# Order of the first expert-weight transfers, and place of one modulation block, in a three-stage block of attention and experts

## The chip, the cores and the metric

One core of a Trainium2 chip runs the whole program. The metric is the device time of one execution in microseconds (us); less is better.

## The reference

For 256 tokens of width 1024 the program computes two layers of a first kind and one of a second kind. Each layer is a mixer (several kinds of attention) followed by a mixture of 16 experts:

```
for l in range(2):
    h = layer_norm(ALPHA * h + mixer(h))
    h = layer_norm(ALPHA * h + grouped_moe(h))
mod = silu(c) @ w_ada + b_ada            # 6 rows of 1024: shifts, scales, gates
x = h + g1 * mixer2(rms(h) * (1 + sc1) + sh1)
x = x + g2 * hier_moe(rms(x) * (1 + sc2) + sh2)
```

An expert layer gives each token two of the 16 experts, and for each expert computes

```
y = y + gate[:, e] * ((silu(h @ w_gate[e]) * (h @ w_up[e])) @ w_down[e])
```

with three 1024x512 float32 weights per expert (2 MiB each, 96 MiB a layer). `w_ada` is 1024x6144 (24 MiB); its product does not depend on `x`, so its 12 column blocks of 512 can be computed anywhere ahead of the third layer.

## The kernel before

**Stages.** The program is one long straight line of instructions per engine, in the order in which the Python code calls them: mixer 1, experts 1, mixer 2, experts 2, mixer 3, experts 3. Below, *expert stage 1, 2, 3* means these three `moe` calls.

**An expert stage** (`moe`, L955) works on eight pairs of experts. The router (`router1`, L856, for stages 1 and 2; `router2` for stage 3) ends in a mask on DVE. TensorE then counts positions (`ppos`, `pcnt`), and `gather(0)` (L979) picks the tokens of the first two pairs into `xT`. At L1127 every engine reads an overflow flag and branches over a rare path (`overflow`, L1124). Then, for each pair, `expand(pr, 0)` multiplies by the gate weights, `expand(pr, 1)` by the up weights (both L1026: 32 matmuls each, written as 64 PE records for a pair), `shrink` by the down weights of the pair before (L1073), and `scatter` adds the result to `yacc`. Inside an `expand` the two experts alternate and `k` runs from 0 to 7; the first half of the weights of an expert holds k = 0 to 3, the second half k = 4 to 7.

**The weight transfers.** `moe_loads` (L916) lists 96 jobs of 1 MiB: for pair 0 gate (jobs 0 to 3), pair 0 up (4 to 7), pair 1 gate (8 to 11), pair 1 up (12 to 15), pair 0 down (16 to 19), pair 2 gate (20 to 23) and so on; in each four the order is first halves of both experts, then second halves. All are issued by the SP queue in list order. `MOE_SEQ` (L39) names for each job the pool its tile comes from, `w` (13 buffers), `b`, `r` or smaller ones; `q`, which only job 3 has, means four pieces of 256 KiB in the small pool `m2` (5 buffers). A transfer whose buffer is still in use waits on the SP queue, and all later transfers wait behind it.

`LATE` (L35) takes a job out of the list and puts it in at another position: job 3 (second half of the second expert's gate in pair 0) stands behind job 21 in stages 1 and 2, and behind job 20 in stage 3. `load(n)` issues the list up to position n: `load(5)` in the mixer (letter `5` of `FILL`), `load(8)` in the third mixer, and `load(22)` or `load(21)` (`MOE_FIRST`, L38) in `moe` ahead of the branch. After the branch the rest follows pair by pair (L1119).

**The buffers of jobs 16 to 19** in stages 1 and 2 come free with the last modulation blocks, because those blocks' weight tiles (`wa`, two of 1 MiB for a block) lie in the same pool `w`.

**The modulation blocks.** `ada` (L1234) is a generator; each step computes one 512-column block: 16 PE matmuls (`pada`, L1244), one ACT copy of the result into the second `wa` tile (L1264), and a small transfer from that tile to DRAM on the POOL queue (L1254). So a block's first `wa` tile is free when the matmuls have read it, the second one when the small transfer has landed. `ada_step` (L1285), at the start of each block, issues a queued follow-up: a small POOL transfer (`adac`, L1272) or two short DVE sums (`total`, L1275).

**The mixer's heads.** `pipe` (L468) goes through 20 attention heads of mixers 1 and 2 and takes filler steps between them (1.1 a head, 22 in all, the rest afterwards). `FILL` (L30) is the order of the fillers of the two mixers: projections (`q k v c f g h`), loads (`5 x a`), one output-projection step for the first 128 tokens (`o`, four matmuls L541), one modulation block (`A`), one output-projection step for the other tokens (`p`). Mixer 1 has four blocks and three `A`, mixer 2 has five blocks and four `A`. The one block that is left is computed after the router by `next(fill, None)` in `run`, followed by `warm(4)` (L117: bf16 matmuls on constants that keep TensorE at work) while the router's chain runs on DVE:

```
            mask, gates = self.router1(pr)
            self.to_tok(h1T, yacc[:, 1, :], 1, ALPHA, "a", "s")
            next(fill, None)
            self.warm(4)
```

Of the kernel before, what the change touches and what calls it, by code (L numbers as in the profile page):

```python
# [26 lines left out]
TABLES = "natural_log_exp_and_others"  # L27
WPOOL = 3
OUT = ("bbbr", (), (0, 1, 2, 3)), ("wwbr", (0, 1), (2, 3))
FILL = ("qkvcfgh5xaoAoAoAopppp", "qkvcfgh5xaoAoAoAoApppp")  # L30
PT1 = "to"
AHEAD = 6
KMC, FLG = (1, 3), 3
EXT, EXT2 = 0, 0
LATE = (3, 21), (3, 20)  # L35
PARTS = {"r": "rr", "x": "r4", "y": "44", "z": "422", "q": "2222"}
GATHER = (1, 3, 5)
MOE_FIRST = 22, 21  # L38
# [9 lines left out]
class Net:  # L48
# [523 lines left out]
    def mixer(self, l, hT, parts, W, ada, mid, tr, load):  # L572
# [64 lines left out]
        def tok(n, dst):  # L637
            pv = self.ps("ptok", "a")
            yield from self.tok3(n, parts, [(pv[:, i * S:(i + 1) * S], i, i == 0) for i in range(2)])
            self.evac(dst.rearrange("p i f -> p (i f)"), pv)  # L640
            yield
# [17 lines left out]
        def fox_qk(n, t, sc):  # L659
            pd = self.ps("pfq", "a")  # L660
            yield from self.proj3(n, parts, [(pd[:, j * S:(j + 1) * S], j * P, P, j == 0) for j in range(2)])
            for j in range(4):
                h = slice(j % 2 * 64, j % 2 * 64 + 64)
                self.evac(fox["QKf"][0:64, t, j, :], pd[h, j // 2 * S:j // 2 * S + S], sc)
            yield
# [5 lines left out]
        def filler():  # L671
# [4 lines left out]
                     "g": lambda: fox_qk("fk", 1, None), "h": lambda: tok("fv", fv)}  # L676
            for step in FILL[l]:
                if step in steps:
# [1160 lines left out]
    def run(self):  # L1839
        A, nc = self.A, self.nc  # L1840
        self.loads()
        c = self.c
        W = self.mixer_loads(0)
        nc.scalar.preload_act_table_set("silu_and_others")
        hT, hp = self.ln_in()
        for l in range(2):
            nc.gpsimd.tensor_scalar(c["qg", l], c["qg", l], 96 ** -0.5, None, op0=ALU.mult)
        self.wstream([(n, W[n]) for n in WSTREAM])
        self.wahead(2)
        tr = iter(())  # L1850
        for l in range(2):
            fill = self.ada(ADA_MX[l], W["ada"])
            h1 = []
            g, b = c["ln1_g", l], c["ln1_b", l]
            pr, parts = [], []

            def mid(xn):

                h1.append(self.big([P, 8, S], "h1T"))
                self.to_T(xn[:, 0], h1[0], g, b, 0)  # L1860
                self.warm(2)
                parts.append(self.parts())
                self.split_hi(xn, parts[0], 0)
                pr.append(self.ps("prt", "o"))
                self.router_mm(h1[0], c["rw"], 16, pr[0], 0)
                self.warm(3)

            We = lambda e: (A["exp_w_gate"][l, e], A["exp_w_up"][l, e], A["exp_w_down"][l, e])
            loads = self.moe_loads(We, MOE_SEQ[0], LATE[0])
            xn = self.mixer(l, hT, hp, W, fill, mid, tr, loads[0])  # L1870
            h1T, pr, parts = h1[0], pr[0], parts[0]
            self.split_lo(xn, parts, 0)
            self.split_hi(xn, parts, 1)
            self.to_T(xn[:, 1], h1T, g, b, 1)
            yacc = self.big([P, 2, D], "yacc")
            self.to_tok(h1T, yacc[:, 0, :], 0, ALPHA, "a", "s")
            self.warm(2)
            self.router_mm(h1T, c["rw"], 16, pr, 1)
            self.split_lo(xn, parts, 1)
            self.dbg(f"h1T{l}", h1T)  # L1880
            mask, gates = self.router1(pr)

            self.to_tok(h1T, yacc[:, 1, :], 1, ALPHA, "a", "s")
            next(fill, None)
            self.warm(4)
            xn2, sts = [], []

            def last(i, n):
                if i == 0 and n == 0:
                    xn2.append(self.big([P, 2, 8, P], "xn2"))  # L1890
                if n == 0:
                    sts.append(self.stats())
                nc.vector.bn_stats(sts[i][:, n, :], yacc[:, i, n * 512:(n + 1) * 512])
                if n == 1:
                    self.ln_rest(yacc, i, self.ln_scale(sts[i], LNE), xn2[0], "aa" if i == 0 else "av")

            self.moe(0, loads, parts, g, b, mask, gates, We, yacc, None, last, fill)
            Wa = self.ada_loads(ADA_TR[l:l + 1])
            W = self.mixer_loads(1) if l == 0 else self.mixer2_loads()
            fill = self.ada(ADA_TR[l:l + 1], Wa, "s", l == 0)  # L1900
            hT = self.big([P, 8, S], "h2T")
            next(fill)
            if l == 0:
                hp = self.hparts()
                self.wstream([(n, W[n]) for n in WSTREAM])
                for i in range(2):
                    self.to_T(xn2[0][:, i], hT, c["ln2_g", l], c["ln2_b", l], i, "ta"[i])
                next(fill)
                for i in range(2):
                    self.hl_tile(hT, hp, i)  # L1910
                tr = fill
                self.wahead(2)
            else:
                sq = self.big([P, 8, S], "sq2")
                self.wstream([(n, W[n]) for n, _ in WIN2_TILES])
                for i in range(2):
                    self.to_T(xn2[0][:, i], hT, c["ln2_g", l], c["ln2_b", l], i, "ta"[i])
                    self.square2(hT, sq, i)
                hp = self.hparts()
                self.wahead(2)  # L1920
                self.rms2(hT, sq, hp, fill)
        We = lambda e: (A["w1_2"][0, e], A["w3_2"][0, e], A["w2_2"][0, e])
        loads = self.moe_loads(We, MOE_SEQ[1], LATE[1])
        xt, parts, h3T, pr, g2b = self.mixer2(hT, hp, W, loads[0])
        self.dbg("x1", xt)
        self.dbg("h3T", h3T)
        mask, gates = self.router2(pr)

        def last(i, n):
            s = slice(n * 512, (n + 1) * 512)  # L1930
            nc.sync.dma_start(self.out[0, i * P:(i + 1) * P, s], xt[:, i, s])

        self.moe(1, loads, parts, self.mcol[:, 4, :], self.mcol[:, 3, :], mask, gates, We, xt, g2b, last)
# [150 lines left out]
```

## Time and profile before

| | |
|---|---|
| median of 3 runs | 1238.4 us (1237.06 to 1243.48) |
| the profiled execution's own time | 1240.28 us |
| its span, first to last instruction | 1238.6 us |
| mean granted TensorE clock | 0.976 |
| TensorE matmul records | 1161.9 us busy, 94% of the span |
| VectorE, ScalarE, GpSimd | 42%, 31%, 20% of the span |
| bytes moved by DMA | 395.46 MB, mean 319 GB/s |
| expert stages, first `expand` to last `shrink` | 191.6 to 401.2, 578.8 to 787.3, 1023.9 to 1230.2 us |

PE is the matmul row of TensorE, PEld its weight loads, DVE, ACT and POOL are the vector, scalar and GpSimd engines, SP the engine that only issues transfers (SPq its queue). A name like `pz<-we,xT` says that the instruction writes tile `pz` and reads `we` and `xT`. In square brackets stands the idle time of the engine before an instruction, and what ended it. PE busy time is modelled (matmuls overlap), so what PE loses is read from its idle times and from how long a known group of matmuls took.

### The profile page before, as it was taken

Reading aid. Unit: us, or ns where it says so; the run is one execution under the profiler, and the core shown is the slowest. Engines: PE = TensorE matmul, PEld = TensorE weight load, DVE = VectorE, ACT = ScalarE, POOL = GpSimd, SP = SyncE. Lnnn points to the kernel's source line nnn. Section 1 sums busy time; section 2 is a strip of 40 time slices with the busy share of each in tenths; the row PEclk is TensorE's granted clock in tenths of the full one; section 3 lists DMA queues with packets and bytes.
Section 4 is the critical chain, followed back from the end, with each engine's and each line's share of the span. In section 5 each row is a group of like instructions: output and inputs, shape, how many; then the busy total and the mean of one; then the engine's idle time right before and its main releaser. Section 6 shows DMA issues by size and latency. Waiting matters only on the chain. (4 is left out here: it accounts for less than half of the span.)

```text
span 1238.6 us, 16671 instructions
## 1 busy us (share of the span) xinstructions
PE 1161.9 (94%) x6366; PEld 673.6 (54%) x6366; DVE 517.1 (42%) x1135; ACT 381.4 (31%) x799; POOL 245.6 (20%) x356
## 2 busy tenths in 40 slices
PE   5999897999999799997999999899899989999997
PEld 4887453434344688645344343489898453434432
DVE  6565351212232756535023221565985360223323
ACT  5545341111111655424011011465464340101100
POOL 4655200000000356320000000132473200000000
PEclk9999898999999999999999999889899998999999
DMA  9814958999999964677999999984354267999995
GB/s 383 338 65 186 399 185 327 408 404 413 414 416 414 419 256 138 248 263 295 378 405 415 413 415 414 418 321 154 114 194 172 102 263 312 415 414 416 415 417 232
DMA packets 77947, 395.46 MB, mean 319 GB/s; under 512 B 7936, under 2 KB 9592, under 8 KB 49440
## 3 DMA queue, kind: packets, MB, share of 16 engines
q1 hardware_dynamic: 73488, 384.66, 78.2%
q0 software_dynamic: 2608, 7.73, 1.6%
q10 hardware_dynamic: 1760, 1.89, 0.5%
q8 instruction: 53, 0.87, 0.3%
q14 instruction: 38, 0.31, 0.1%
HBM read 389.41 MB, written 6.51 MB: 320 GB/s over the span
## 5 line engine op out<-in xcount | busy, mean ns | idle before, releaser
L1026 PE MATMUL pz<-we,xT 128*64 128x512 f32 x1536 | 343.9, 604 | 19.8 <-DMA we<-in_exp_w_gate 12.3
L1026 PEld LDWEIGHTS pz<-we,xT 128*64 128x64 f32 x1536 | 110.8, 139 | 239.6 <-issue 217.8
L1073 PE MATMUL py<-wd,aT 128*64 128x512 f32 x768 | 171.1, 593 | 0.9 <-DMA wd<-in_w 0.9
L1035 DVE TENSOR_TENSOR act<-sil,pz 128x512 f32<-128x512 f32 x24 | 16.5, 688 | 327.8 <-PE pz L1026 302.8
L1050 POOL TENSOR_SCALAR m_ge<-m_s 64x1 f32<-64x1 f32 x48 | 11.9, 247 | 586.5 <-DVE m_s L1045 339.9
L1073 PEld LDWEIGHTS py<-wd,aT 128*64 128x64 f32 x768 | 56.6, 137 | 110.2 <-issue 105.6
L1030 ACT ACTIVATE sil<-pz 128x512 f32<-128x512 f32 x24 | 14.3, 597 | 217.8 <-PE pz L1026 217.8
L1079 ACT ACTIVATE yh<-py,m_ge 128x512 fp32r<-128x512 f32 x32 | 22.0, 688 | 187.6 <-PE py L1073 187.6
L1080 DVE SCALAR_TENSOR_TENSOR yl<-py,m_ge,yh 128x512 fp32r<-128x512 f32 x32 | 24.0, 751 | 96.3 <-ACT yh L1079 96.3
L541 PE MATMUL pout<-w_o,oT 128*128 128x512 f32 x128 | 58.2, 602 | 0.0
L986 PE MATMUL pg<-G,xhi 128*128 128x256 f32 x192 | 47.8, 290 | 2.0 <-DVE G L975 2.0
L448 POOL TENSOR_SCALAR E<-E,r 128x128 f32<-128x128 f32 x40 | 31.6, 791 | 77.4 <-DVE r L444 77.2
L986 PE MATMUL pg<-G,xlo 128*128 128x256 f32 x192 | 46.7, 283 | 0.0
L1085 ACT ACTIVATE yh<-yf 128x512 fp32r<-128x512 f32 x16 | 10.1, 631 | 104.0 <-DVE yf L1084 104.0
L1099 PE MATMUL psc<-yh,GT 128*128 128x512 f32 x96 | 39.3, 410 | 1.1 <-ACT yh L1085 0.8
L1101 DVE TENSOR_TENSOR yacc<-yacc,psc 128x512 f32<-128x512 f32 x64 | 40.1, 680 | 0.0
L1099 PE MATMUL psc<-yl,GT 128*128 128x512 f32 x96 | 38.5, 401 | 1.3 <-DVE yl L1080 0.6
L541 PEld LDWEIGHTS pout<-w_o,oT 128*128 128x128 f32 x128 | 23.8, 194 | 26.0 <-issue 25.6
L986 PEld LDWEIGHTS pg<-G,xhi 128*128 128x128 f32 x192 | 36.7, 191 | 2.4 <-issue 1.6
L986 PEld LDWEIGHTS pg<-G,xlo 128*128 128x128 f32 x192 | 36.8, 191 | 0.0
L442 ACT ACTIVATE E<-s,nm 128x128 f32<-128x128 f32 (+1 forms) x48 | 20.2, 421 | 47.9 <-DVE nm L441 45.6
L1244 PE MATMUL pada<-wa,cz 128*32 128x512 f32 x192 | 24.2, 618 | 8.4 <-DVE yacc L1101 4.5
(512 smaller groups left out, 2122.4 us busy)
## 6 DMA issues: line engine op xcount, KB each, us to landing
wd<-in_exp_w_down SPq DMA_DIRECT2D x58, 1024.0 KB, 16.3
we<-in_exp_w_up SPq DMA_DIRECT2D x54, 1024.0 KB, 13.1
we<-in_w SPq DMA_DIRECT2D x52, 1024.0 KB, 15.0
we<-in_exp_w_gate SPq DMA_DIRECT2D x48, 1024.0 KB, 11.7
wd<-in_w SPq DMA_DIRECT2D x29, 1024.0 KB, 15.3
wa<-in_p_ada SPq DMA_DIRECT2D x24, 1024.0 KB, 15.2
we<-in_exp_w_gate SPq DMA_DIRECT2D x28, 512.0 KB, 13.7
we<-in_w SPq DMA_DIRECT2D x22, 512.0 KB, 14.8
```

The lines of the kernel that those rows point to most:

```text
L442: nc.scalar.activation(E[:, s], sc[:, s], AF.Exp, bias=nm[:, i:i + 1], accum_out=sm[:, i:i + 1])
L448: self.nc.gpsimd.tensor_scalar(E[:, 0:P], E[:, 0:P], r[:, 0:1], None, op0=ALU.mult)
L541: self.nc.tensor.matmul(acc, oT[:, cc, i * P:(i + 1) * P], w[cc][:, n * 512:(n + 1) * 512], start=(cc == 0), stop=(cc == 7), skip_group_ch ...
L986: nc.tensor.matmul(pg[:, :256], part[:, i, k, :], Gq[q][:, i].rearrange("p e s -> p (e s)"), start=(n == 0), stop=(n == 3))
L1026: nc.tensor.matmul(pz[64 * e:64 * e + 64, :], x[:, k, o + 64 * e:o + 64 * e + 64], w[e][k], start=(k == 0), stop=(k == 7), skip_group_chec ...
L1035: nc.vector.tensor_mul(a, st[pr].pop("sil"), pz)
L1073: nc.tensor.matmul(py[n][64 * e:64 * e + 64, :], aT[:, f, 64 * e:64 * e + 64], w[e][f][:, n * 512:(n + 1) * 512], start=(f == 0), stop=(f ...
L1079: nc.scalar.activation(yh[:, s], py[n], AF.Copy, scale=ge)
L1080: nc.vector.scalar_tensor_tensor(yl[:, s], py[n], ge, yh[:, s].bitcast(F32), op0=ALU.mult, op1=ALU.subtract)
L1099: nc.tensor.matmul(pt, GT[:, i * P:(i + 1) * P], y[:, s], start=(j == 0), stop=(j == 1), skip_group_check=True)
L1101: nc.vector.tensor_tensor(yacc[:, i, s], yacc[:, i, s], pt, op=ALU.add)
L1244: nc.tensor.matmul(pa[32 * k:32 * k + 32, :], c["cz"][:, 4 * k4 + k:4 * k4 + k + 1].to_broadcast([P, 32]), w[:, k, :], start=(k4 == 0), st ...
```

## The change

In the two lists `FILL` and `LATE`, and in `run`:

```
-FILL = ("qkvcfgh5xaoAoAoAopppp", "qkvcfgh5xaoAoAoAoApppp")
+FILL = ("qkvcfgh5xaoAoAoAoApppp", "qkvcfgh5xaoAoAoAoAApppp")
...
-LATE = (3, 21), (3, 20)
+LATE = (3, 16), (3, 16)
...
             self.to_tok(h1T, yacc[:, 1, :], 1, ALPHA, "a", "s")
-            next(fill, None)
-            self.warm(4)
+            self.warm(11)
```

The four pieces of job 3 are issued behind job 16, ahead of jobs 17 to 21 (stage 3: 17 to 20). The last modulation block of mixers 1 and 2 becomes one more `A` among the heads, ahead of the first `p`, and in its old place stand seven more matmuls of `warm`. All tiles, pools and sums stay as they are.

## Rows read from the trace of the kernel before

**Rows 1.** The page, costliest groups: matmuls of `expand`; after the bar busy, mean ns, idle

```profile
L1026 PE MATMUL pz<-we,xT 128*64 128x512 f32 x1536 | 343.9, 604 | 19.8 <-DMA we<-in_exp_w_gate 12.3
```

**Rows 2.** Timeline of PE at the first `expand` of stages 1, 2, 3

```profile
191.59 4.50 PE L1026 MATMUL pz<-we,xT 128*64 128x512 f32 x18 [0.35 <-ACTq L1128]
202.47 12.79 PE L1026 MATMUL pz<-we,xT 128*64 128x512 f32 x46 [6.38 <-DMA we<-in_exp_w_gate]
...
578.78 4.48 PE L1026 MATMUL pz<-we,xT 128*64 128x512 f32 x18 [1.23 <-PEq L1128]
589.22 12.27 PE L1026 MATMUL pz<-we,xT 128*64 128x512 f32 x46 [5.97 <-DMA we<-in_exp_w_gate]
...
1023.91 16.81 PE L1026 MATMUL pz<-we,xT 128*64 128x512 f32 x64 [5.52 <-issue]
```

**Rows 3.** SP's waits, 171 to 197 us and 557 to 584 us: total, times, longest

```profile
SPq L114 <- PE pada L1244: 6.4, 1, 6.4
SPq L114 <- DMA ada<-wa: 6.1, 1, 6.1
...
SPq L114 <- DMA ada<-wa: 6.5, 1, 6.5
```

**Rows 4.** Timeline of SP: the four down tiles of pair 0 in stage 1

```profile
176.61 14.29 SPq L114 DMA_DIRECT2D wd<-in_exp_w_down  x4
```

**Rows 5.** Issues by L114 from 191.9 to 194 us: the four pieces

```profile
L114 SPq DMA_DIRECT2D we<-in_exp_w_gate x4: 452/473/1228, 192.0 to 193.6; - x4
...
DMA to landing us min/median/max: 10.5/10.6/11.5
```

**Rows 6.** Stretches: PE, PEld, DVE, ACT, POOL busy (x), clock, DMA share, GB/s

```profile
187.00:192.00 5.00, 4.52 (x34) 4.14 (x36) 2.86 (x9) 2.87 (x5) 0.15 (x1) 1.00 0.48 139
202.50:215.30 12.80, 12.80 (x47) 3.95 (x47) 0.00 (x0) 0.60 (x1) 0.00 (x0) 0.82 0.91 331
216.00:396.00 180.00, 179.90 (x894) 77.43 (x896) 44.97 (x89) 26.34 (x42) 4.69 (x17) 1.00 1.01 411
576.00:582.00 6.00, 4.77 (x29) 2.74 (x29) 2.19 (x9) 2.41 (x3) 0.26 (x1) 1.00 0.63 230
...
589.00:601.50 12.50, 12.28 (x47) 3.79 (x47) 0.00 (x0) 0.60 (x1) 0.00 (x0) 0.85 0.90 337
...
1024.00:1030.00 6.00, 6.00 (x16) 1.98 (x18) 0.00 (x0) 0.00 (x0) 0.00 (x0) 0.52 0.25 90
...
1014.20:1018.00 3.80, 3.80 (x31) 3.75 (x31) 2.12 (x6) 1.74 (x4) 0.10 (x1) 1.00 1.03 409
```

**Rows 7.** The chain that ended last: one undisturbed pair of `expand`, one `shrink`

```profile
1042.24 13.88 PE pz L1026 x64
1056.13 6.87 PE py L1073 x32
```

**Rows 8.** Timeline of PE: the last `shrink` but one of stage 1

```profile
383.73 7.59 PE L1073 MATMUL py<-wd,aT 128*64 128x512 f32 x32
```

**Rows 9.** Timeline of PE: after the router of stage 1; ends of mixers 1 and 2

```profile
182.86 1.92 PE L1244 MATMUL pada<-wa,cz 128*32 128x512 f32 x16
184.71 1.05 PE L121 MATMUL warm<-onesb 128*128 128x512 bf16 x4
186.08 0.17 PE L964 MATMUL ppos<-p_mask,tri 128*128 128x16 bf16 x1 [0.32 <-DVE p_mask L911]
...
156.30 15.72 PE L541 MATMUL pout<-w_o,oT 128*128 128x512 f32 x36
...
542.48 17.43 PE L541 MATMUL pout<-w_o,oT 128*128 128x512 f32 x40
```

**Rows 10.** Tile `wa` in mixer 1, 116 to 142.6 us: issues and landing

```profile
L114 SPq DMA_DIRECT2D wa<-in_p_ada x4: 397/428/477, 116.1 to 117.7; - x4
...
DMA to landing us min/median/max: 5.6/16.3/24.6
```

**Rows 11.** DMA queues from 1021.3 to 1022.6 us: kind, packets, MB, share

```profile
q8 instruction: 1, 0.02, 5.3%
```

## The prediction

> **What bounds the kernel now.** I read the page's costliest groups first, then PE's timeline where the largest group stood idle, then SP's waits, then stretches of DMA rate, and last the chain. The `expand` matmuls are the largest group, and of their 19.8 us of idle time 12.3 us end with a gate weight [rows 1]. The timeline puts these into two places: in stages 1 and 2 PE starts `expand(0, 0)`, does 18 records (k = 0 to 3 and a little), and then stands for 6.38 and 5.97 us until job 3 is there [rows 2]. After the stop the granted clock of the stretch is 0.82 and 0.85 [rows 6], a mix of the levels 2.4 and 1.2 GHz. The whole pair of `expand` took from 191.59 to 215.26 and from 578.78 to 601.49 us, 23.7 and 22.7 us, where an undisturbed one takes 13.88 us [rows 2, 7]. So PE loses 9.8 and 8.8 us there.
>
> Why job 3 is late is on the SP queue: it stands behind two down tiles that wait for the last modulation block, one for its matmuls (6.4 us in stage 1), one for its small transfer to DRAM (6.1 and 6.5 us) [rows 3]; the four down tiles together take 14.29 us to issue [rows 4]. The pieces go out at 192.0 to 193.6 us and need 10.5 to 11.5 us to land: 202.5 us, which is when PE goes on [rows 2, 5].
>
> The other bound is the stream of weights. From 216 us to the end of stage 1 it runs at 411 GB/s, DMA share 1.01, without a break [rows 6]. PE needs less time for a pair than the stream, starts far ahead in loaded weights, and uses the lead up: the last `shrink` but one takes 7.59 us instead of 6.87 us, so it already waits a little for its weights [rows 7, 8]. At the end of an expert stage both are level. Hence what PE gains at its start it keeps only as far as the stream gains too. The stream does have holes to fill, just where SP stood.
>
> **The change, part by part.**
>
> *Job 3 behind job 16.* Job 16 goes out at 176.61 us [rows 4]; the pieces follow and, at the slowest landing of their row, 11.5 us, are there near 190 us [rows 5]. PE asks for them about 4 us after its first record at 191.59. They need four small buffers that the heads used, and the heads are over when the long output projection starts at 156.30 us [rows 9]. So the stop goes in stages 1 and 2. Late next: nothing for 30 us (up weights and pair 1 were issued earlier than job 16).
>
> *The block among the heads.* It removes both SP waits of rows 3: its two tiles are free some 30 us before jobs 18 and 19 ask. PE gets 1.92 us more in each mixer [rows 9], and the fillers behind it move one step back; one `p` more is left for after the heads. Mixer 2 already has this form against mixer 1 (40 records of L541 instead of 36), and that costs 17.43 - 15.72 = 1.71 us [rows 9]; with the block itself against the four-matmul step it displaces, 1.75 us a mixer, all on PE's path, which has no idle time there to take it. Its tiles: issued by 117.7 us, landed after 24.6 us at the most, 142.3 us [rows 10]; in mixer 1 the new `A` comes near 144 us, a margin of only 2 us. The ACT copy, the POOL transfer and, in mixer 2, two DVE sums ride along; by the page those engines are less than half busy. I take 0 for them, 0.5 us a mixer if that cover fails.
>
> *After the router.* PE loses the block (1.92 us) and gets seven more warm matmuls, 1.05 / 4 = 0.26 us each or less, 1.8 us. PE waited 0.32 us for the router's mask there [rows 9]; DVE sets that time, so this is worth 0, and at most some tenths either way.
>
> *What the stream gains.* In stage 1 it moved 139 GB/s from 187 to 192 us and 331 GB/s from 202.5 to 215.3 us, where 411 is its pace: (1 - 139/411) x 5 = 3.3 us, (1 - 331/411) x 12.8 = 2.5 us, together 5.8 us of hole. In stage 2, 230 GB/s over 6 us and 337 GB/s over 12.5 us: 2.6 + 2.3 = 4.9 us [rows 6]. The first hole of each is SP's wait, the second the places that PE, standing still, did not give back. Both close. The stream starts 1.75 us later because the mixer ends later. Gain: 5.8 - 1.75 = 4.0 and 4.9 - 1.75 = 3.2 us, 7.2 us. Bounds: if only the first holes close, 3.3 + 2.6 - 3.5 = 2.4 us; if PE alone counted, 9.8 + 8.8 - 3.5 = 15.1 us. I take 7.2, since the row at the end of the stage shows PE already waiting for the stream.
>
> *Stage 3.* Nothing waited for job 3 there; PE's 64 records start late, at 1023.91 after 5.52 us idle ended by "issue", and run in 16.81 us at a clock of 0.52 until 1030 [rows 2, 6]. What ended the idle time shows in the DMA queues: one instruction packet, 1021.3 to 1022.6 us [rows 11], code that PE fetches behind the branch. The change adds 7 matmuls with their weight loads a mixer, 14 records, so 28 ahead of this branch; whatever place in the code asks for that packet then lies 28 records earlier before the branch. At the pace of `gather` (62 records in 3.8 us [rows 6]) that is 1.7 us. The trace does not show where the asking is done, so the bounds are 0 and 7 us (all idle time and half of the slow clock gone); I take 1.5 us, which the stream here gets in full, since it waits for PE (90 GB/s from 1024 to 1030 us [rows 6]).
>
> *Sum.* 7.2 + 1.5 = 8.7 us off 1240.3 us, the profiled execution's own time: 1231.6 us. That execution lies 1.9 us above the median, so against the median: 1238.4 - 8.7 = **1229.7 us**.
>
> **The rivals.**
>
> *PE's code takes the place of the weights: slower.* At the branch PE stood 0.35, 1.23 and 5.52 us in the three stages [rows 2]; the long one came with the stream at full rate (409 GB/s just ahead of it), the short one with 139 GB/s [rows 6]. The change fills the queue in stages 1 and 2 too. If the code then comes as late as in stage 3, PE stands 5.2 and 4.3 us longer at the branch, starts at the low clock (16.81 against 13.88 us, 2.9 us more), and the stream gets the hole of stage 3, (1 - 90/409) x 6 = 4.7 us from 1024 to 1030, and a second one as in stage 1, 2.5 us, for those it lost: 7.2 instead of 5.8 and 4.9 us. That is 1.4 + 2.3 + 3.5 for the mixers = 7.2 us slower, 1245.6 us. It decides once PE's idle time at both branches passes some 4 us. Against it: the 14 and 28 records more also move the asking forward. The Trainium skill ("Runtime: NRT & Kernel Launch", Instruction fetch mechanics) has the rule for this: code comes in 16 KiB blocks of 256 instructions, fetched ahead in sequence, and a taken branch out of the loaded blocks waits for a DMA. By that rule the packet of rows 11 is such a block, and the trace agrees in its size, 0.02 MB. Chance 0.05.
>
> *The holes close only in part* (pieces issued, but their buffers or the buffers of jobs 20 and 21 free later than I think, or the block costs more among the heads, such as 2 to 4 us for a `wa` tile that lands late): gain 0 to 5 us, 1233 to 1238 us. For: the margin of 2 us. Chance 0.15.
>
> *PE's gain counts more than the stream's*, or stage 3 loses most of its 5.52 us: 12 to 16 us, 1222 to 1226 us. For: the stream's end is only level with PE's. Against: share 1.01 for 180 us. Chance 0.18.
>
> *The change does not do what it says*: job 3's place in the list moves, but the pieces' buffers come free only with `gather`, so they go out near 190 us as before. Then the block alone works: the first holes close, 2.4 us, 1236 us. Chance 0.04.
>
> **How the numbers follow.** The forecast has 0.58. A measurement of this kernel tells 0.5% or 6.2 us from no change, so faster means under 1232.2 us. Faster: most of the forecast (0.54 of 0.58; the rest ends just short of the bound) and the third rival (0.18), with a fifth of the partial case (0.03): 0.75. Slower by 6.2 us: the code rival at its full price, 0.03. The rest, 0.22, is the same. The range leaves out the far ends of the third rival and the code rival: 1221 to 1237 us.
>
> **What would show it.** Right: PE's 64 records of pair 0 in one piece of about 14 us in stages 1 and 2, no "DMA we" before them; the pieces out right behind the first down tile; no SP wait on `pada` or `ada`; over 380 GB/s from 187 to 215 us; 40 and 44 records of L541 after the heads; the last `shrink`s of stages 1 and 2 waiting 1 to 3 us longer. Wrong: an idle time over 4 us at the branch in stage 1 or 2, a wait of PE for the last `wa` tiles among the heads, or a `shrink` that waits longer than PE gained.

## The result, and the profile after

The changed kernel takes 1226.47 us (median of 4 runs, 1225.23 to 1228.42), the kernel before beside it 1237.83 us: a ratio of 0.9897, 95% interval 0.9869 to 0.9926 (the two medians alone give 0.9908). The profiled execution of the changed kernel took 1228.42 us, its span is 1226.8 us. The forecast was 1229.7 us.

The page's costliest groups, after:

```profile
L1026 PE MATMUL pz<-we,xT 128*64 128x512 f32 x1536 | 338.2, 598 | 8.4 <-PEq L1128 8.0
...
L1073 PE MATMUL py<-wd,aT 128*64 128x512 f32 x768 | 172.3, 593 | 2.0 <-DMA wd<-in_exp_w_down 2.0
```

The idle time of `expand` fell from 19.8 to 8.4 us, and none of it ends with a gate weight any more [rows 1]. 8.0 us of it now end with the branch of L1128 on PE's own sequencer. The `shrink`s wait 2.0 us for down weights. The timeline of PE at the first `expand` of the three stages says where (start, us, ..., idle before and what ended it):

```profile
192.53 15.56 PE L1026 MATMUL pz<-we,xT 128*64 128x512 f32 x64 [2.13 <-PEq L1128]
576.55 13.95 PE L1026 MATMUL pz<-we,xT 128*64 128x512 f32 x64 [2.03 <-PEq L1128]
1014.23 15.65 PE L1026 MATMUL pz<-we,xT 128*64 128x512 f32 x64 [3.82 <-PEq L1128]
```

All three pairs run in one piece; the stops of 6.38 and 5.97 us are gone. Stage 1's pair takes 15.56 us and not 13.95, at a granted clock of 0.66 from 192 to 197 us; in the second profile of the same kernel (below) it takes 13.95 us. But the idle time at the branch grew from 0.35 and 1.23 us to 2.13 and 2.03 us in stages 1 and 2, and fell from 5.52 to 3.82 us in stage 3 [rows 2]. The timeline of SP's queue in stage 1:

```profile
171.94 5.36 SPq L114 DMA_DIRECT2D we<-in_exp_w_up  x3
177.36 0.42 SPq L114 DMA_DIRECT2D wd<-in_exp_w_down  x1
177.89 2.23 SPq L114 DMA_DIRECT2D we<-in_exp_w_gate  x4
180.22 2.06 SPq L114 DMA_DIRECT2D wd<-in_exp_w_down  x3
184.93 13.69 SPq L114 DMA_DIRECT2D we<-in_exp_w_gate  x4
```

The pieces go out right behind the first down tile, and the other three down tiles, whose group took 14.29 us [rows 4], follow in 2.06 us. No wait of SP on `pada` or `ada` is left. Stretches of the changed kernel (PE, PEld, DVE, ACT, POOL busy, clock, DMA share, GB/s):

```profile
187.00:192.00 5.00, 3.40 (x29) 3.20 (x27) 3.05 (x10) 3.54 (x5) 0.12 (x1) 1.00 1.03 418
202.50:215.30 12.80, 12.49 (x63) 4.69 (x60) 1.80 (x5) 0.60 (x1) 0.62 (x2) 1.00 1.00 413
...
576.00:582.00 6.00, 5.45 (x26) 2.30 (x28) 0.13 (x2) 0.00 (x0) 0.24 (x1) 1.00 1.03 419
589.00:601.50 12.50, 12.21 (x62) 4.58 (x60) 1.80 (x5) 1.20 (x2) 0.63 (x2) 1.00 1.01 415
1015.00:1018.40 3.40, 3.40 (x10) 1.20 (x8) 0.00 (x0) 0.00 (x0) 0.00 (x0) 0.50 0.73 280
```

Where 139, 331, 230 and 337 GB/s stood, there are 418, 413, 419 and 415 [rows 6]: the four holes are closed. Stage 3 still starts at half clock (0.50 to 1018.4 us), but its first pair takes 15.65 us where it took 16.81 with 6 us at 0.52. At the ends of stages 1 and 2 PE waits for the stream (timeline, the last `shrink` but one; the first line is stage 2 of the kernel before):

```profile
769.96 7.47 PE L1073 MATMUL py<-wd,aT 128*64 128x512 f32 x32
...
376.57 8.00 PE L1073 MATMUL py<-wd,aT 128*64 128x512 f32 x32
...
758.98 1.89 PE L1073 MATMUL py<-wd,aT 128*64 128x512 f32 x8
761.41 1.07 PE L1073 MATMUL py<-wd,aT 128*64 128x512 f32 x2 [0.55 <-DMA wd<-in_exp_w_down]
763.96 5.36 PE L1073 MATMUL py<-wd,aT 128*64 128x512 f32 x22 [1.48 <-DMA wd<-in_exp_w_down]
```

Stage 1's takes 8.00 us instead of 7.59 [rows 8], stage 2's 10.34 us (758.98 to 769.32) instead of 7.47; in the second profile they take 9.95 and 9.71 us. The `shrink`s ahead of them take 7.04 us each on this timeline. The block's price, from the timeline of PE at the ends of mixers 1 and 2, and behind the router of stage 1:

```profile
155.33 17.43 PE L541 MATMUL pout<-w_o,oT 128*128 128x512 f32 x40
...
537.75 19.15 PE L541 MATMUL pout<-w_o,oT 128*128 128x512 f32 x44
...
181.92 2.57 PE L121 MATMUL warm<-onesb 128*128 128x512 bf16 x11
185.24 0.17 PE L964 MATMUL ppos<-p_mask,tri 128*128 128x16 bf16 x1 [0.75 <-DVE p_mask L911]
```

40 and 44 records of L541, 1.71 and 1.72 us more each [rows 9], and the mask is still waited for.

For the rest of the text the span is cut into three parts: A from the start of the long output projection in mixer 1 to the end of stage 1, B from there to the end of stage 2 (mixer 2 and stage 2), C to the end of stage 3 (mixer 3 and stage 3). The ends are those of the last `shrink`s. In us, one profiled execution each:

| kernel | A | B, of it mixer 2 | C | idle at the branch, stages 1, 2, 3 |
|---|---|---|---|---|
| before | 244.92 | 386.11, 177.56 | 442.82 | 0.35, 1.23, 5.52 |
| changed | 239.13 | 384.76, 182.09 | 439.11 | 2.13, 2.03, 3.82 |
| changed, again | 239.60 | 382.93, 180.91 | 438.66 | 2.25, 2.62, 3.78 |
| pieces alone | 240.21 | 382.63, 178.63 | 440.95 | 2.33, 2.30, 5.47 |
| pieces alone, again | 240.05 | 381.72, 178.47 | 441.51 | 2.65, 2.21, 5.51 |
| block alone | 240.26 | 383.96, 180.28 | 438.01 | 3.18, 1.94, 3.60 |
| stage 3's pieces alone | 244.57 | 389.68, 179.49 | 440.07 | 0.35, 1.03, 5.26 |
| before + 28 records | 244.71 | 388.31, 179.44 | 438.54 | 0.69, 0.99, 3.69 |
| changed + 96 records | 238.93 | 384.28, 178.60 | 436.75 | 0.35, 0.22, 2.73 |
| pieces + 124 records | 240.51 | 381.41, 176.46 | 438.20 | 0.35, 0.22, 2.73 |
| the same, again | 238.66 | 381.25, 178.16 | 436.81 | 0.35, 0.22, 2.73 |
| pieces + 210 records | 239.52 | 383.99, 177.98 | 437.17 | 0.35, 0.22, 2.73 |
| changed + 2 MB a stage | 244.31 | 392.29, 184.63 | 439.79 | 2.57, 2.50, 3.78 |

From before to changed: A -5.79, B -1.35, C -3.71 us, and the output projection starts 0.97 us sooner (156.30 to 155.33), which is no work of the edits: the first modulation block of mixer 1, ahead of all of them, already starts at 117.61 us instead of 119.00. Together that is 11.82 us of span. Between executions of equal code, part A varies by some 0.2 to 1.9 us and B by up to 1.8, C by up to 1.4 us (the three pairs named "again"), so single parts are read to about 1 to 2 us only; totals are the medians below. The kernel before has one profile, but stages 1 and 2 are the same in it, in stage 3's pieces alone and, but for the records, in before + 28 records.

### The profile page after: what moved, and what is told of

The parts are those of the page before. It is cut to its first block, busy times and chain, and to the rows that moved or that the text cites. A ratio compares the mean times of both kernels' runs of the same rounds, so it can differ in the third digit from the quotient of the medians.

```text
span 1226.8 us, 16706 instructions
## 1 busy us (share of the span) xinstructions
PE 1161.3 (95%) x6380; PEld 673.1 (55%) x6380; DVE 517.6 (42%) x1135; ACT 380.8 (31%) x799; POOL 246.3 (20%) x356
## 5 line engine op out<-in xcount | busy, mean ns | idle before, releaser
L1026 PE MATMUL pz<-we,xT 128*64 128x512 f32 x1536 | 338.2, 598 | 8.4 <-PEq L1128 8.0
L1026 PEld LDWEIGHTS pz<-we,xT 128*64 128x64 f32 x1536 | 111.2, 138 | 221.9 <-issue 213.3
L541 PE MATMUL pout<-w_o,oT 128*128 128x512 f32 x128 | 58.3, 604 | 0.0
L541 PEld LDWEIGHTS pout<-w_o,oT 128*128 128x128 f32 x128 | 24.0, 195 | 27.1 <-issue 25.6
```

The lines of the kernel that those rows point to most:

```text
L541: self.nc.tensor.matmul(acc, oT[:, cc, i * P:(i + 1) * P], w[cc][:, n * 512:(n + 1) * 512], start=(cc == 0), stop=(cc == 7), skip_group_ch ...
L1026: nc.tensor.matmul(pz[64 * e:64 * e + 64, :], x[:, k, o + 64 * e:o + 64 * e + 64], w[e][k], start=(k == 0), stop=(k == 7), skip_group_chec ...
```

## The experiments

Two theories. **A: in stages 1 and 2 the stream of weights sets the end**, so what counts is holes in it, and PE's own stops cost nothing beyond them. **B: PE's idle time at the branch is a wait for a packet of its code**, whose time depends on where the branch lies in PE's code and on how full the DMA queue is. The first four kernels shared their runs of the kernel before (1240.03 us, 24 runs), the next four theirs (1239.21 us, 11 runs), the last three theirs (1239.21 us, 17 runs). In kernels that add records, lines stand 7 later (L1033 is L1026), with 2 MB more 2 later. Where records are added or counted ahead of a branch, a matmul and its weight load are two; the x64 of a line of the timeline counts matmuls alone.

**The pieces alone.**

```
-LATE = (3, 21), (3, 20)
+LATE = (3, 16), (3, 16)
```

> Only the place of job 3's pieces moves (ahead of the waiting down tiles, in all three stages); the last modulation block stays after the router. Theory A, the stream sets the end of stages 1 and 2: PE's stop (6.38 and 5.97 us) goes, the pieces also fill most of the hole that the two waits of SP leave, and the heads pay nothing, so stage 1 gains 4 to 5 us and stage 2 as much: 8 to 10 us less, about 1229 us, as good as the whole change up to its part in stage 3. Rival, both edits are needed: SP still waits 6 us, the hole ahead of PE's start stays, and the two stages together gain under 5 us: 1233 to 1236 us. For stage 3, theory B (PE's idle time at the branch hangs on where the branch lies in the blocks of PE's code) expects 5.5 us idle there, as before, since no PE instruction is added; its rival, that the earlier pieces shorten it, expects 3.8 us.

Measured: 1228.0 us, ratio 0.9916 (0.9888 to 0.9944), and 1227.55 us, 0.9902 (0.9881 to 0.9922), when run again. PE, the queue of SP and one stretch:

```profile
193.89 15.57 PE L1026 MATMUL pz<-we,xT 128*64 128x512 f32 x64 [2.33 <-PEq L1128]
...
575.47 15.65 PE L1026 MATMUL pz<-we,xT 128*64 128x512 f32 x64 [2.30 <-PEq L1128]
...
1015.54 16.05 PE L1026 MATMUL pz<-we,xT 128*64 128x512 f32 x64 [5.47 <-PEq L1128]
```

```profile
177.46 2.40 SPq L114 DMA_DIRECT2D we<-in_exp_w_gate  x4
179.95 12.35 SPq L114 DMA_DIRECT2D wd<-in_exp_w_down  x3
```

```profile
187.00:192.00 5.00, 4.11 (x32) 3.94 (x32) 2.90 (x8) 2.56 (x5) 0.44 (x2) 1.00 0.99 381
192.00:197.00 5.00, 3.11 (x8) 1.13 (x10) 1.03 (x7) 0.98 (x1) 0.25 (x1) 0.68 0.74 295
```

SP still stands (12.35 us for three down tiles), but with 1 MB more in the queue by then the hole is 0.4 + 1.4 us, where it was 3.3, and the second hole is gone with PE's stop. Without the block among the heads this is as fast as the whole change. In stage 3 the pieces went out just as early and the idle time stayed at 5.47 us: the earlier pieces are not what shortened it.

**The block alone.** The new `FILL` and `warm(11)` with the old `LATE`:

```
-FILL = ("qkvcfgh5xaoAoAoAopppp", "qkvcfgh5xaoAoAoAoApppp")
+FILL = ("qkvcfgh5xaoAoAoAoApppp", "qkvcfgh5xaoAoAoAoAApppp")
...
-            next(fill, None)
-            self.warm(4)
+            self.warm(11)
```

> Only the last modulation block moves among the heads (and seven more warm matmuls follow the router); job 3's pieces stay behind job 21. Theory A: SP's waits go, the stop of PE in stages 1 and 2 shrinks from 6 to 2 to 4 us since the pieces go out some 3 us earlier, the heads pay 1.75 us a mixer: 0 to 3 us less from the stages. Theory B: 28 PE records more ahead of the third branch, so its idle time falls from 5.5 to 3.8 us and the stage gains 2 to 4 us. Together 3 to 6 us less, 1232 to 1235 us. If the earlier pieces, not the records, were what shortened the idle time of stage 3, it stays at 5.5 us and the kernel is at 1235 to 1238 us.

Measured: 1230.17 us, 0.9929 (0.9901 to 0.9958), better than expected.

```profile
200.94 10.51 PE L1026 MATMUL pz<-we,xT 128*64 128x512 f32 x46 [1.19 <-DMA we<-in_exp_w_gate]
...
584.31 10.52 PE L1026 MATMUL pz<-we,xT 128*64 128x512 f32 x46 [2.26 <-DMA we<-in_exp_w_gate]
...
1014.59 15.65 PE L1026 MATMUL pz<-we,xT 128*64 128x512 f32 x64 [3.60 <-PEq L1128]
```

```profile
183.86 15.87 SPq L114 DMA_DIRECT2D we<-in_exp_w_gate  x8
```

With SP not waiting, job 20 and 21 and then the pieces follow from 183.86 us on, the stop shrinks to 1.19 and 2.26 us, and part A is as short as with the pieces alone. So **the two edits close the same holes**: alone they save 11.7 to 12.0 us and 9.9 us of median, together 11.1 to 11.4. Stage 3's idle time is 3.60 us with the old place of the pieces: the records ahead of the branch did that.

**Stage 3's pieces alone.** Only the second entry changes:

```
-LATE = (3, 21), (3, 20)
+LATE = (3, 21), (3, 16)
```

> Only stage 3's pieces of job 3 move. Theory B: no change, PE's idle time ahead of stage 3 stays at 5.5 us with 6.8 us of half clock behind it, 1238 us. Rival, the earlier pieces are what shortened it in the changed kernel: 3.8 us idle and 3 to 4 us less, 1234 us.

Measured: 1239.29 us, 0.9993 (0.9977 to 1.0009). As theory B has it:

```profile
1023.90 15.67 PE L1026 MATMUL pz<-we,xT 128*64 128x512 f32 x64 [5.26 <-issue]
```

The pair behind the wait took 15.67 us here, with the wait nearly as long as in the kernel before, where it took 16.81: the time of that pair varies by itself.

**28 PE records more, nothing else.**

```
+    def pad(self, n):
+        ps = self.ps("pad", "o")
+        for _ in range(n):
+            self.nc.tensor.matmul(ps[:, 0:1], self.c["onesb"], self.c["oneb"], start=True, stop=True,
+                                  skip_group_check=True)
...
         W = self.mixer_loads(0)
+        self.pad(14)
```

> The kernel before with 14 tiny matmuls (one column each) more at the program's start, where PE waits for its first weights anyway; nothing else moves. They add 28 PE records ahead of every branch, as the change does ahead of the third. Theory B: PE's idle time ahead of stage 3 falls from 5.5 to 3.8 us, the half clock behind it gets shorter, and the kernel is 2 to 4 us faster, 1234 to 1236 us; the idle times of stages 1 and 2 (0.35 and 1.23 us) fall by some tenths at most. Rival, the place in the code does not matter: 5.5 us as before, 1238 us.

Measured: 1237.07 us, 0.9982 (0.9968 to 0.9995): 3.0 us of median less, 2.2 us by the ratio.

```profile
1022.63 15.45 PE L1033 MATMUL pz<-we,xT 128*64 128x512 f32 x64 [3.69 <-PEq L1135]
```

5.52 became 3.69 us, within 0.2 us of the changed kernel, by 14 tiny matmuls at the other end of the program. In stage 1 the idle time did not fall but rose to 0.69 us, which was not expected.

**The changed kernel with 96 records more.** The same `pad`, with 48 matmuls, on the changed kernel.

> The changed kernel with 48 tiny matmuls (96 PE records) more at the program's start, where PE stands idle for 7.6 us. In all runs so far PE's first expand record starts 1.66 us after the end of the code packet ahead of it. Theory B: the packet is asked for at a fixed place in PE's code, now 96 records, some 5.9 us, earlier before each branch, so PE's idle times of 2.13, 2.03 and 3.82 us fall to about 0.35 us, which is what the value of the branch itself takes; no half clock behind the third. Stage 3 gains 3.5 us and some 1.7 us of clock, stages 1 and 2 gain little, since the stream sets their end: 4 to 7 us less than the changed kernel, 1220 to 1223 us. Rival, the packet is asked for only when the branch is taken: idle times as they were, 1226 to 1228 us.

Measured: 1227.44 us, 0.9907 (0.9889 to 0.9924), beside 1228.15 us, 0.9919 (0.9899 to 0.9940), for the changed kernel run again. The idle times fell, so theory B stands; the time hardly did.

```profile
191.15 13.95 PE L1033 MATMUL pz<-we,xT 128*64 128x512 f32 x64 [0.35 <-ACTq L1135]
...
573.26 13.95 PE L1033 MATMUL pz<-we,xT 128*64 128x512 f32 x64 [0.22 <-ACTq L1135]
...
1012.87 13.95 PE L1033 MATMUL pz<-we,xT 128*64 128x512 f32 x64 [2.73 <-ACTq L1135]
...
755.72 3.08 PE L1080 MATMUL py<-wd,aT 128*64 128x512 f32 x8
759.43 1.07 PE L1080 MATMUL py<-wd,aT 128*64 128x512 f32 x2 [0.63 <-DMA wd<-in_exp_w_down]
761.98 7.06 PE L1080 MATMUL py<-wd,aT 128*64 128x512 f32 x22 [1.48 <-DMA wd<-in_exp_w_down]
771.85 7.09 PE L1080 MATMUL py<-wd,aT 128*64 128x512 f32 x32
```

In stage 2 PE starts at 573.26 us, the changed kernel beside it at 576.80, 3.54 us later; the last `shrink` of that stage starts at 771.85 here and at 771.74 there. The whole lead is spent in the last `shrink` but one: it takes 13.32 us here (755.72 to 769.04) and 9.71 us in the changed kernel beside it, stretched by waits for down weights. In stage 3 a floor shows: 2.73 us, ended by ACT's sequencer at the branch. The timeline of ACT says what ACT did, here from the next kernel's second run, with the idle time of PE from 1005.70 to 1008.43:

```profile
1006.58 0.21 ACT L1822 ACTIVATE r_s<-r_s 128x8 f32<-128x8 f32 x1 [0.76 <-DVE r_s L1821]
1007.53 0.23 ACT L1829 ACTIVATE r_s<-r_s 128x32 f32<-128x32 f32 x1 [0.74 <-DVE r_s L1828]
```

PE's first record behind the branch waits for ACT, and ACT gets to the branch only after two steps of the router's gates, which it exchanges with DVE. That was hidden behind the code. So of the 3.8 us at this branch only 1.05 could be gained. (Behind the same 2.73 us the pair takes 13.95 us here and 15.65 us in the next kernel, at granted clocks of 1.00 and 0.72 in its first 6 us.)

**The pieces alone with 124 records more.** `LATE` as above and `pad(62)`, on the kernel before.

> The pieces alone (no block among the heads), with 62 tiny matmuls (124 PE records) more at the program's start. Theory B: the idle times of 2.33, 2.30 and 5.47 us fall to about 0.35 us each; stage 3 gains 5.1 us and some 2 us of clock, stages 1 and 2 up to 1 us each: 6 to 9 us less than the pieces alone, 1219 to 1222 us. If the block among the heads is needed for more than SP's waits, it stays above the changed kernel with its 96 records.

Measured: 1223.67 us, 0.9872 (0.9847 to 0.9897). Run again beside the pieces alone:

> The pieces alone with the 124 PE records more at the start, once more. From the runs so far: PE starts 2.0, 2.1 and 2.7 us sooner at the three branches; if stages 1 and 2 are ended by the stream, only the third counts in full, with up to 2 us of half clock and up to 1 us from an earlier start of the mixer behind: 2.5 to 5 us less than the pieces alone beside it, 1222 to 1225 us. If PE's start counted everywhere, 7 us and more: under 1221 us.

1223.03 us, 0.9872 (0.9848 to 0.9896), against 1227.55 us: 4.5 us less.

```profile
191.70 13.95 PE L1033 MATMUL pz<-we,xT 128*64 128x512 f32 x64 [0.35 <-ACTq L1135]
...
573.32 13.95 PE L1033 MATMUL pz<-we,xT 128*64 128x512 f32 x64 [0.22 <-ACTq L1135]
...
1008.43 15.65 PE L1033 MATMUL pz<-we,xT 128*64 128x512 f32 x64 [2.73 <-ACTq L1135]
```

In the two profiles part C falls by 4.70 us, from 441.51 to 436.81. Parts A and B give 1.4 and 0.5 us, within what equal code varies by, though PE stood 2.3 and 2.0 us less at those branches. This version is faster than both kernels: 1223.67 us beside 1228.15 us for the changed kernel in the same set of runs, the intervals of their ratios just apart.

> The pieces alone once more, beside the next one on the same chip: 1227 to 1229 us, idle times at the branches near 2.3, 2.3 and 5.5 us.

(The pieces alone, second run: the figures above.)

**The pieces alone with 210 records more.** `pad(105)`.

> The pieces alone, with 105 tiny matmuls (210 PE records) more at the start. With 256 records to a packet, 210 more are the same as 46 fewer where the asking lies far enough ahead: Theory B expects 2.8 us more idle at the branches of stages 1 and 2 (2.33 and 2.30 become about 5 us) and 0.35 us in stage 3, which was 5.47. So the long idle time changes its place. It prices the prediction's rival, code in the way of PE at stages 1 and 2: by the prediction's own sum each would cost 5 us and more against no idle time; by the stream theory the stages hide a good part, 0 to 3 us each. Together 1221 to 1229 us. Rival, the place does not matter: 1228 us with idle times as in the pieces alone.

Measured: 1222.18 us, 0.9871 (0.9847 to 0.9895). The long idle time did not come back to stages 1 and 2 as I had worked out.

```profile
187.28 1.07 PE L1033 MATMUL pz<-we,xT 128*64 128x512 f32 x2 [0.35 <-ACTq L1135]
190.04 13.89 PE L1033 MATMUL pz<-we,xT 128*64 128x512 f32 x62 [1.68 <-issue]
...
569.52 1.50 PE L1033 MATMUL pz<-we,xT 128*64 128x512 f32 x5 [0.22 <-ACTq L1135]
572.01 13.09 PE L1033 MATMUL pz<-we,xT 128*64 128x512 f32 x59 [0.99 <-issue]
```

What came is a stop behind the branch, 2 and 5 matmuls into `expand`: 1.68 and 0.99 us, with the next code packet landing 1.3 us before PE goes on in stage 1. So it counts where the branch lies among the packets, but where the asking is done I had placed wrong, and the price of a code wait over 4 us at these branches was not measured.

**The changed kernel again.** No edit.

> The changed kernel once more, beside the others on the same chip: 1226 to 1228 us, idle times at the branches near 2.1, 2.0 and 3.8 us. It shows how much of mixer 2's 4.5 us longer time comes back: the block's 1.75 us and the 0.8 us at the branch should be there again, the 2 us of low clock at the mixer's start may not.

Measured: 1228.15 us, 0.9919 (0.9899 to 0.9940). Mixer 2 takes 180.91 us, 3.35 more than before, where the first profile had 4.53. The wait at the branch is 1.4 us of it (2.62 for 1.23), the block 1.7 us; so there is nothing else to explain in this run.

**2 MB more in each of stages 1 and 2.** The changed kernel with transfers that nothing reads:

```
                    k = d
+                if SEQ is MOE_SEQ[0] and j in (41, 53):
+                    self.nc.sync.dma_start(self.dp.tile([P, m, src.shape[2]], F32, name="xtra"), src)
```

> The changed kernel with two more transfers of 1 MB on SP in each of stages 1 and 2, from a down weight to a scratch tile in DRAM that nothing reads (jobs 41 and 53). Theory A, the stream sets the end of these stages: 2.5 us a MB, so each stage ends 5 us later, by longer waits of PE for the last weights; 10 us more than the changed kernel, about 1237 us, more if a transfer to DRAM takes longer than one to SBUF. Rival, PE sets the end and the stream has time to spare: 0 to 2 us more, 1227 to 1230 us.

Measured: 1239.8 us, 1.0001 (0.9987 to 1.0014), 11.65 us above the changed kernel's second set of runs: the extra 4 MB cost what the change had gained. Part A is 4.71 us longer than in the changed kernel's second profile, stage 2 alone 5.64 us (207.66 for 202.02), and stage 1's last `shrink` but one shows the waits (timeline of PE):

```profile
380.44 1.93 PE L1075 MATMUL py<-wd,aT 128*64 128x512 f32 x6 [1.42 <-DMA wd<-in_exp_w_down]
383.01 1.07 PE L1075 MATMUL py<-wd,aT 128*64 128x512 f32 x2 [0.64 <-DMA wd<-in_exp_w_down]
385.57 5.36 PE L1075 MATMUL py<-wd,aT 128*64 128x512 f32 x22 [1.49 <-DMA wd<-in_exp_w_down]
```

That is 2.4 and 2.8 us a MB: theory A, near to the number. The extra transfers also write to DRAM, which the weights don't; what that adds was not measured apart. Stage 3, where nothing differs from the changed kernel, shows again that the pair's time varies (timeline of PE; 15.65 and 15.47 us in the changed kernel's two profiles, behind the same wait):

```profile
1026.59 16.87 PE L1028 MATMUL pz<-we,xT 128*64 128x512 f32 x64 [3.78 <-PEq L1130]
```

(Mixer 2 is 3.7 us longer too, with a granted clock of 0.88 from 400.8 to 430 us and 0.92 from 560 to 586; I don't put that down to the transfers.)

## Why the prediction was right, and where its terms were off

It said 8.7 us by closing holes in the stream; measured were 11.4 us of median, and the mechanism is the one it gave. Stages 1 and 3 were priced too low; stage 2 came out near its price, as far as single profiles can tell. Two of its readings need a word: the 6.87 us of an undisturbed `shrink` come from the chain, where the timeline, from which the 7.59 us are, has 7.04, so PE's wait at the end of stage 1 was 0.55 us and not 0.72; and the last `shrink`s but one grew by 0.4 and 2.9 us in the first profile, 2.4 and 2.2 in the second, for the 1 to 3 us that it named. By its steps:

- **Job 3 behind job 16.** Right. The pieces went out at 177.9 to 179.7 us with 7.7 to 8.3 us to land, so at 185.6 to 188.0 us, before PE had even begun the 18 records ahead of them.
- **The block's price.** Right: 1.71 and 1.72 us for 1.75. The block's tiles were not late either: it ran at 143.00 us with no wait ahead of it.
- **After the router, 0.** Right: the wait for the mask is 0.75 us instead of 0.32.
- **Stage 1, 4.0 us.** Part A gave 5.79 and 5.32 us in the two profiles, 5.4 us between the means of three executions without the edits and two with them. The holes closed as priced. What the sum left out is that the stream behind them also got faster: 411 GB/s from 216 to 380 us in the kernel before and in the two kernels that leave stages 1 and 2 alone, 413 to 415 in all the others. (1 - 411/414) x 164 = 1.2 us. Why is open: the profile shows DMA shares of 1.01 and 1.02 and no more.
- **Stage 2, 3.2 us.** Part B gave 1.35 us in the first profile and 3.18 in the second. The sum had taken the 1.75 us of the block as all that mixer 2 pays. It pays the code wait at its end too (0.8 to 1.4 us). And the profiled execution of the kernel before had a short mixer 2: stage 3's pieces alone and the 28 records do nothing there, and need 179.49 and 179.44 us for 177.56. Against the mean of these three, 388.0 us, B gave 3.3 and 5.1 us, 4.2 on average.
- **Stage 3, 1.5 us.** The term that was furthest off. C gave 3.71 and 4.16 us against the one profile of the kernel before, which is the longest of its kind: the four executions with 5.3 to 5.5 us idle at this branch have 440.07 to 442.82 us in C, the five with 3.6 to 3.8 us 438.01 to 439.79, 2.5 us less on average. The idle time fell by 1.70 us, just the 1.7 that 28 records at `gather`'s pace were worth. The pair behind it also ran in 15.65 instead of 16.81 us, but that is not shown to follow from the shorter wait: 15.67 us stand behind 5.26 us idle and 16.87 behind 3.78. The 28 records alone gave 2.2 us by the interval's ratio, with neither edit made: so some 2 us of the change's gain come not from what it says but from where its instructions put the branch.
- **PE's gain counts more than the stream's**: the size came near that rival's range (12 to 16 us off), its reason is not borne out. With 96 records more PE started 1.9 us sooner within part A, which got 0.7 us shorter, and 3.5 us sooner in stage 2, which ended no sooner; 2 MB more cost 4.7 and 5.6 us a stage.
- **The change does not do what it says**: priced at 2.4 us for the block alone. Run alone, the block gave 9.9 us of median. Two things were missing in that price: with SP not waiting, the pieces behind job 21 come sooner too, so that the stop shrinks to 1.19 and 2.26 us and the second holes nearly close (385 GB/s from 202 to 216 us, where it was 341), and the records ahead of the third branch work without the pieces.
- **PE's code takes the place of the weights**: its mechanism came true and its price did not. The idle times of stages 1 and 2 rose by 1.8 and 0.8 us, below the 4 us that it named, since the queue was full where the packet was asked for; and at that size the stream hides them. What the prediction held against this rival, that the 14 and 28 records more move the asking forward, does not show in these stages: with the pieces alone, so without the records, PE stood 2.33 and 2.65 us in stage 1 and 2.30 and 2.21 in stage 2, with them (changed, twice, and block alone) 2.13, 2.25 and 3.18, and 2.03, 2.62 and 1.94. Why 28 records help in stage 3 and not here is open.

The code wait itself, in the packets of queue q8 (us against the end of PE's last record ahead of the branch):

| kernel, stage | code packet ends | first `expand` | between |
|---|---|---|---|
| before, 3 | +4.06 | +5.52 | 1.46 |
| changed, 1 | +0.46 | +2.13 | 1.67 |
| changed, 3 | +2.16 | +3.82 | 1.66 |
| pieces alone, 3 | +3.82 | +5.47 | 1.65 |
| before + 28, 3 | +2.03 | +3.69 | 1.66 |
| changed + 96, 3 | -5.36 | +2.73 (ACT) | - |

The fetch is asked for ahead of the branch, not by it: with 96 records more the packet is there 5.36 us before PE's last record ahead of the branch. PE's branch instruction itself (booked under PEld; duration in ns) took 4.37 us in stage 3 of the changed kernel and 0.31 us with the pieces alone and 124 records more:

```profile
L1128 PEldq COMPARE_BRANCH  x1: 4370/4370/4370, 1009.5 to 1009.5; - x1
...
L1135 PEldq COMPARE_BRANCH  x1: 313/313/313, 1004.8 to 1004.8; - x1
```

A fuller queue delays it: in stage 1 the packet ended 1.67 us before PE's last record in the kernel before and 0.66 us after it with the pieces alone, at the same place in the code. The Trainium skill ("Runtime: NRT & Kernel Launch", Instruction fetch mechanics) says that blocks of code are fetched ahead in sequence and that a taken branch out of them waits for a DMA; the trace agrees with both, and shows further that the wait can be moved out of the way, down to the 0.35, 0.22 and 2.73 us that ACT sets. Which place in the code asks is not settled.

## What to carry to other kernels

Where the transfers set the end of a stage, add up the holes in their rate, not the idle time of the engine that waits for them; two edits that close the same hole don't add up, so each is run alone, and a megabyte that nothing reads shows in one run whether the stream is the bound. A change of the number of instructions ahead of a branch moves that branch in the code and can give or take a few us by itself: before a gain is put down to an edit, run the same number of idle instructions without it. Here 62 tiny matmuls where PE had nothing to do, with one half of the change, beat the whole of it.

## What the runs showed that I had not expected

- In all runs together the code packet set PE's start at 25 branches. At 23 of them PE's first record came 1.64 to 1.68 us after the end of the packet, at two (stage 3 in the kernel before and with stage 3's pieces alone) 1.46 and 1.35 us. At these two the branch instruction was through in 0.32 us and PE stood behind it; why it is so there is open.
- Where the pieces of 256 KB land, the DMA engines can be full at a lower rate: from 182 to 187 us the changed kernel moves 345 GB/s at a share of 0.99, the kernel before, with whole tiles, 398 at 1.01. But it does not always come with the pieces: in the kernel before they land from 197 us on, and from 197 to 202 us it moves 395 GB/s at 1.00.
- The granted clock falls to half in some executions at places that no edit touches, as at the start of mixer 2: the 16 `pada` records there took 1.92 us in the kernel before, 2.83 us in the first profile of the changed kernel and 3.61 us in its second, each time behind 2.23 or 2.24 us of idle time. The length of the idle time ahead does not tell it either: 3.18 us (block alone, stage 1) and 2.25 us (changed, second profile, stage 1) left the clock at full, 2.13 us (changed, first profile, stage 1) did not.
